# Modulation's last products and the router's set-up moved behind the final norm, its two factors computed in one chain, x parked from ScalarE's queue

## The chip, the core and the metric

The kernel runs on one core of a Trainium2 chip. The metric is the device time of one execution in microseconds (us); a kernel is run several times and the median is given. The core has five engines that run side by side, each with its own instruction stream in a fixed order: TensorE (matrix products, PE, with its weight loads PEld), VectorE (DVE), ScalarE (ACT), GpSimd (POOL) and SyncE (SP). DMA transfers are issued from the queues of SP, ScalarE and GpSimd. [...]

## The reference

All data is float32; 256 tokens of width 1024. A first block has two layers, each with a mixer and a convolutional FFN, and ends with an RMS norm. A second block follows: it is modulated by six vectors from `c`, has a mixer with sparse attention and an RWKV branch, and a mixture of 32 experts. The parts that matter here, shortened:

```
x = x + conv_ffn(rms_norm(x, norm_ffn[1]), ...)        # last FFN of the first block
h = rms_norm(x, norm_final)                             # the final norm
mod = silu(c) @ ada_w + ada_b
sh1, sc1, gt1, sh2, sc2, gt2 = split(mod, 6)
xn = rmsnorm(h, mix_norm_g) * (1 + sc1) + sh1           # the norm that follows at once
proj = xn @ w_in                                        # projections of the second mixer
h = h + gt1 * (merged @ w_out)
xn2 = rmsnorm(h, moe_norm_g) * (1 + sc2) + sh2
h = h + gt2 * hier_moe(xn2, router weights, expert weights)
```

So two norms stand one behind the other: the final norm of the first block, whose result `h` is also the residual of the second block, and the modulated norm before `proj`. `sh2`, `sc2` and `gt2` are needed only behind the second mixer: the first two by the router and the experts, `gt2` when the experts' results are added.

## The kernel before, in words

Tokens lie on the partitions in two tiles of 128 (`x[0]`, `x[1]`), or features lie on the partitions and tokens along the free dimension (`hT`, 8 blocks of 128 features). Large products are made of three fp32r products of a high and a low part each (`mm3`, L272 to L274); the weights are loaded from SP (`load_raw`, L241), and split into the parts by ScalarE and VectorE (`split_act`, L305 and L306).

*The end of the last FFN.* It accumulates in four PSUM banks of the pool `pc`, first the left 512 columns for both token tiles, then the right ones. When a half is complete, `ending` adds it to x (L420), `final_half` multiplies by `norm_final` (L1382) and turns the result into feature blocks on TensorE (L377), and the sums of squares of this product and of x are taken on ScalarE (L334).

*The two norms in one.* `final_norms` makes from the two sums of a token the factor of both norms together: three small instructions (L1396 to L1398) and `newton`, an inverse square root by three Newton steps. It is called for one column at a time, for each of the two token tiles; for one column a step has two instructions (L318, L322), for several columns three (L320, L321, L322). `factor_rows` brings the factors into a row: for each token tile a diagonal (L353, one buffer for both) and a product with ones (L354), then a copy (L355). For each of the 8 feature blocks follow L1407 (VectorE: block by gain by row), L1408 (ScalarE: shift added, rounded to the high part) and L1409 (VectorE: the low part). Last come the two tiles of x itself (L1411), with a factor of their own (`rms`), which the second block needs as its residual.

*Modulation.* The weights of the six vectors are loaded and mostly summed up on VectorE during the first block (`mod_load`). `mod_steps` makes the last products of what is ready: for the shift `sh2` 8 small products for each half (L828) and an addition (L830), for the gate `gt2` one product of one row by 512 columns for each half (L817), an addition of the bias (L818) whose row is loaded from SP into one buffer (L816), and a store of the result (L819). `final_norms` calls it between the Newton steps and `factor_rows`.

*Router's set-up.* `router_setup` loads the router's weights from GpSimd's queue, multiplies them by the shift (8 products, L1523), adds the bias and spreads the row over the partitions (L1524, L1526, L1528), and scales the weights (L1529). It is called between the first block and the second mixer.

*The second mixer.* `second_mixer` closes the PSUM pools and opens others (2, 3 and 3 banks instead of 4 and 4), stores both tiles of x to memory from SP (L1441, the parked x), and starts with the projections: the low-rank inputs of RWKV (`rwkv_low`), the index of the sparse attention, key, receptance and value of RWKV, in between the index mask on VectorE, then `rwkv_prep`.

*What sets the order.* The program above is not the order on the engines. When the kernel is built, a planner orders the instructions of each engine by the time at which it thinks their inputs and places ready, and among ready ones by their position in the program. Instructions stand far from their place in the program: the constant that L1535 makes in `router_setup` is computed at 1.4 us. At run time each engine keeps the planned order and waits where an input is late.

Of the kernel before, what the change touches and what calls it, by code (L numbers as in the profile page):

```python
# [17 lines left out]
NT = 2  # L18
TT = (slice(0, 128), slice(128, 256))
# [71 lines left out]
def view(v, dims, dtype):  # L91
    if dtype not in (F32, F32R):
        v = v.bitcast(dtype)
    names = "abcde"[:len(dims)]
    if len(dims) > 1:
        left = f"({' '.join(names)})"
        v = v.rearrange(f"p {left} -> p {' '.join(names)}", **dict(zip(names, dims)))
    return v


def flat(t):
    n = len(t.shape) - 1
    names = " ".join("abcde"[:n])
    return t.rearrange(f"p {names} -> p ({names})") if n > 1 else t


class Net:
# [1279 lines left out]
    def final_norms(self, p, ss, banks):  # L1387

        nc, x, xg, sg = self.nc, self.x, self.xg, self.sg
        hi, lo = self.hT  # L1390
        stt = nc.vector.scalar_tensor_tensor
        rs = []
        for t in range(NT):

            w, y, u = (self.stile(1, f"rms2_{n}") for n in "wyu")
            nc.vector.tensor_scalar(w, ss[t][0], ss[t][1], 1e-6, op0=ALU.add, op1=ALU.mult)  # L1396
            nc.vector.tensor_scalar(w, w, 1e-12 * D, sg[t][0], op0=ALU.add, op1=ALU.add)
            nc.vector.tensor_scalar(w, w, sg[t][1], 0.5 / D, op0=ALU.add, op1=ALU.mult)  # L1398
            self.newton(y, w, u)
            rs.append(y)  # L1400
        self.mod_steps()
        gcol, shcol = self.mod_cols(0, 1, self.mix_g)
        rows = self.factor_rows(rs, p)
        for k in range(8):
            ps, sh = banks[k // 2][:, k % 2], shcol[:, k:k + 1]
            full = p.tile([128, S], name="full", bufs=2)
            stt(full, ps, gcol[:, k:k + 1], rows, op0=ALU.mult, op1=ALU.mult)  # L1407
            nc.scalar.activation(hi[:, k], full, AF.Identity, bias=sh)  # L1408
            stt(lo[:, k], full, sh, hi[:, k].bitcast(F32), op0=ALU.add, op1=ALU.subtract)  # L1409
        for t in range(NT):  # L1410
            nc.scalar.activation(x[t], xg[t], AF.Copy, scale=self.rms(ss[t]))  # L1411
        p.drop(*list(p.tags))

    def gate(self, gate, i, blocks=range(0, 8, 2)):

        for f in blocks:
            ps = self.psum("pg")
            self.feats([ps], self.w2(2888 + 1024 * i + 128 * f, 256), self.hT)
            self.nc.scalar.activation(flat(gate[:, f:f + 2]), ps, AF.Tanh, scale=0.5)
# [13 lines left out]
    def second_mixer(self):  # L1433
        nc, tc, A, x = self.nc, self.tc, self.A, self.x
        tt, stt = nc.vector.tensor_tensor, nc.vector.scalar_tensor_tensor
        self.open_psum(pg=2, pc=3, ps=3)
        self.ring(0, 4)

        park = self.dram.tile([S, D], F32, name="x_park")
        for t in range(NT):  # L1440
            nc.sync.dma_start(park[TT[t]], x[t])  # L1441
        self.base.drop("x0", "x1")
        self.par1.drop(*list(self.par1.tags))
        with ExitStack() as es:
            E = lambda: es.enter_context(self.scope())
            p, z, pa, pg, pc = E(), E(), E(), E(), E()
            split = lambda n: (lambda y: (y[:, 0], y[:, 1]))(p.tile([128, 2, 4, S], F32R, name=n))
            oa = split("oa")
            room = self.part(p, 10240, "room")
            first, second, third = (Arena(self.af.tiles, room.gaps[0][0] + o, n)  # L1450
                                    for o, n in ((0, 7168), (7168, 3072), (8192, 2048)))
            both = z.tile([128, 4096], name="rw_KRB")
            pb = Scope(self, self.part(pa, 5760, "attention"))
            gates = [pg.tile([128, 8, S], name=f"gate{i}") for i in range(2)]
            qkv, bias = pb.tile([128, 3, 1024], name="qkv"), pb.tile([128, 384], name="bias")
            self.ring(3, 4)
            KR, KB = view(both[:, :2048], (2, 4, S), F32), view(both[:, 2048:], (16, 2, 64), F32)
            v, g, bon = (z.tile([128, 4, S], name=f"rw_{n}") for n in ("v", "g", "bon"))
            with self.scope(first) as zz, self.scope(second) as px:
                sg, k, a = (zz.tile([128, 4, S], name=f"rw_{n}") for n in ("sg", "k", "a"))  # L1460
                self.rwkv_low(sg, a, g, first)
                mask = self.index_mask(px, *self.index_in(px), bias)
                self.rwkv_proj(k, 1, "pg")
                next(mask)
                self.rwkv_proj(KR[:, 1], 0, "pg")
                next(mask)
                self.rwkv_proj(v, 2, "pg")
                fe = self.rwkv_prep(p, zz, KR, KB, bon, k, v, sg, a)
            qT, kT, vn = self.qkv(qkv, third)
            with self.scope(room) as pr:  # L1470
                ops = self.rwkv_pairs(pr, pc, KR, KB)
                z.drop("rw_KRB")
                orw = split("orw")
                self.rwkv_bonus(bon, v)
                self.gate(gates[0], 0, range(0, 8, 2))
                self.rwkv_chain(pc, ops, v, fe, lambda i, Y, junk: self.rwkv_out(i, Y, junk, bon, g, orw))
                self.attention(pb, qT, kT, vn, bias, oa)
                self.gate(gates[1], 1)
                pa.drop(*list(pa.tags))
                for _ in self.branch(A["w_branch_attn_2"][0], oa, gates[0]):  # L1480
                    pass
            pc.drop(*list(pc.tags))
            z.drop("rw_g", "rw_v", "rw_bon")
            p.drop("room", "oa")
            self.par2.drop(*list(self.par2.tags))
            self.ring(8, 4)
            self.x = x = [self.base.tile([128, D], name=f"x{t}") for t in range(NT)]
            for t in range(NT):
                nc.sync.dma_start(x[t], park[TT[t]])
            last = Scope(self, self.part(p, 2 * D, "last"))  # L1490
            gt1 = self.bcast_row(self.mod[0], last.tile([128, D], name="gt1"))
            self.late = [(a, a + n) for a, n in p.tags["last"][1]]
            m = self.hT
            for j in self.branch(A["w_branch_rwkv_2"][0], orw, gates[1]):
                sl = slice(j, j + 2)
                ga, gr = (flat(y[:, sl]) for y in gates)
                tt(ga, ga, gr, ALU.add)
                mh, ml = (flat(y[:, sl]) for y in m)
                nc.scalar.activation(mh, ga, AF.Copy, scale=0.5)
                stt(ml, ga, 0.5, mh.bitcast(F32), op0=ALU.mult, op1=ALU.subtract)  # L1500
            acc = [[self.bank(), self.bank()], [self.bank(), self.psum()]]
            done, ss = self.ending(acc, lambda n: None, gt1, last)
            for i in range(2):
                mi = tuple(y[:, 4 * i:4 * i + 4] for y in m)
                self.out_proj(acc, self.items(mi, A["w_out_2"][0], 4 * i, 4), i == 0, done if i == 1 else None)
            return ss
# [254 lines left out]
def build(nc, tc, A, out):  # L1761
    with ExitStack() as ctx:
        net = Net(nc, tc, ctx, A, out)
        net.first_block()
        net.router_setup()
        ss = net.second_mixer()
        net.finish_blocks()
        net.moe(ss)
# [18 lines left out]
```

## Time and profile before

| | |
|---|---|
| median of 3 runs | 1501.56 us (1499.7 to 1502.51) |
| profiled execution | 1502.12 us, of which the span from the first to the last instruction 1500.4 |
| mean granted clock | 0.950 |
| busy: PE, DVE, ACT, POOL | 1371.2, 852.7, 615.2, 32.2 us |
| end of the last FFN's products | 727.3 us |
| first projection of the second mixer | 740.8 us |
| first expert products | 1047.8 us |

Times in the trace count from the span's start. A row of the timeline gives the start, the duration from the first to the last of merged instructions, the engine, the line of the kernel, the operation, what it writes and reads, shapes, and in brackets how long the engine was idle before it and what ended that. One fp32 product is shown as two records. Tiles are called by their storage: `arena` and `arena_r` hold almost all of them, `pc`, `ps` and `pg` are PSUM.

### The profile page before, as it was taken

The page shows a single profiled execution, that of the slowest core. Times are in us where ns is not written, and L with a number is a line of the kernel's source. Part 1 is how long each engine was busy: PE and PEld are TensorE (multiplying, and loading weights), DVE is VectorE, ACT ScalarE, POOL GpSimd, SP SyncE. Part 2 cuts the span into 40 slices and gives each one's busy share as a digit, 9 for nine tenths or more (in the row PEclk, how much of TensorE's full clock was granted, in tenths as well). Part 3 has the DMA queues.
Part 4 walks back from the last instruction along what each step waited for, and adds up shares of the span by engine and source line. Part 5 has one row for each costly group of instructions (what it writes and reads, how often), then busy time and mean ns, then how long its engine had stood idle before and what let it go on. Part 6 is the DMA issues. An engine that isn't in the chain of part 4 may idle for free.

```text
span 1500.4 us, 22885 instructions
## 1 busy us (share of the span) xinstructions
PE 1371.2 (91%) x9085; PEld 1042.1 (69%) x9085; DVE 852.7 (57%) x1628; ACT 615.2 (41%) x955; POOL 32.2 (2%) x63
## 2 busy tenths in 40 slices
PE   7999999999999899999999899998978878879785
PEld 6778999999998689999798688887413313234131
DVE  5796798778788789878859742775201101101011
ACT  6644555556688555555575544552100000000000
POOL 3000000000001000000000100001000000000000
PEclk9999999999999999999899795999999989999998
DMA  9898586555555578563243352487999999999997
GB/s 318 282 327 277 158 274 215 187 187 160 170 182 184 172 272 275 187 191 109 72 153 113 99 121 86 170 336 308 390 421 420 420 420 421 421 421 419 421 419 253
DMA packets 165573, 391.18 MB, mean 261 GB/s; under 512 B 19440, under 2 KB 101100, under 8 KB 141780
## 3 DMA queue, kind: packets, MB, share of 16 engines
q1 hardware_dynamic: 153124, 383.64, 70.2%
q10 hardware_dynamic: 11136, 4.53, 1.3%
q0 software_dynamic: 1200, 1.49, 0.4%
q8 instruction: 73, 1.20, 0.3%
q14 instruction: 40, 0.33, 0.1%
HBM read 386.19 MB, written 3.43 MB: 260 GB/s over the span
## 4 chain that ended last, share of the span: by engine, by line
PE 58%; DMA 29%; DVE 7%; ACT 4%; issue 2%; SPq 0%; POOL 0%; DVEq 0%; ACTq 0%
DMA arena<-expert_w_gate 12%; PE ps L272 9%; PE ps L273 9%; PE ps L274 9%; DMA arena_w<-expert_w_gate 7%; DMA arena_w<-expert_w_down 6%; PE pc L273 5%; PE pc L272 5%; PE pc L274 5%; DMA arena<-expert_w_down 3%; PE pg L272 2%; PE pg L274 2%; PE pg L273 2%; DVE arena_r L306 2%; ACT arena_r L305 1%
## 5 line engine op out<-in xcount | busy, mean ns | idle before, releaser
L305 ACT ACTIVATE arena_r<-arena 128x1024 fp32r<-128x1024 f32 (+2 forms) x330 | 328.9, 1008 | 287.1 <-PE ps L273 73.1
L306 DVE TENSOR_TENSOR arena_r<-arena,arena_r 128x1024 fp32r<-128x1024 f32 (+2 forms) x330 | 376.9, 1154 | 119.2 <-ACT arena_r L305 115.8
L272 PE MATMUL ps<-arena_r,arena_r 128*128 128x256 f32 (+2 forms) x1192 | 353.7, 297 | 1.0 <-DVE arena L818 1.0
L273 PE MATMUL ps<-arena_r,arena_r 128*128 128x256 f32 (+2 forms) x1192 | 352.9, 296 | 1.1 <-DVE arena_r L306 1.1
L274 PE MATMUL ps<-arena_r,arena_r 128*128 128x256 f32 (+2 forms) x1192 | 352.4, 296 | 0.6 <-DVE arena_r L306 0.6
L272 PEld LDWEIGHTS ps<-arena_r,arena_r 128*128 128x128 f32 (+1 forms) x1192 | 229.3, 192 | 10.4 <-issue 3.5
L273 PEld LDWEIGHTS ps<-arena_r,arena_r 128*128 128x128 f32 (+1 forms) x1192 | 229.2, 192 | 7.2 <-DVE arena_r L306 1.5
L274 PEld LDWEIGHTS ps<-arena_r,arena_r 128*128 128x128 f32 (+1 forms) x1192 | 229.2, 192 | 5.6 <-DVE arena_r L306 0.8
L1709 PE MATMUL pc<-arena 128*32 128x512 f32 x576 | 144.4, 672 | 34.1 <-DMA arena<-expert_w_up 18.9
L272 PE MATMUL pc<-arena_r,arena_r 128*128 128x512 f32 x344 | 136.0, 399 | 5.3 <-ACT arena_r L305 3.4
L273 PE MATMUL pc<-arena_r,arena_r 128*128 128x512 f32 x344 | 135.9, 395 | 0.4 <-DVE arena_r L306 0.4
L274 PE MATMUL pc<-arena_r,arena_r 128*128 128x512 f32 x344 | 134.2, 393 | 0.0
L1709 PE MATMUL pc<-arena_w,arena 128*32 128x512 f32 x448 | 117.4, 663 | 15.8 <-DMA arena_w<-expert_w_gate 9.8
L1716 DVE TENSOR_TENSOR arena<-arena,pc 128x512 f32<-128x512 f32 x8 | 5.5, 688 | 204.6 <-PE pc L1709 204.6
L1692 ACT ACTIVATE arena<-ps,mod_col,moe_g 128x128 f32<-128x128 f32 x32 | 14.7, 458 | 246.1 <-DVE arena L1694 246.1
L1709 PEld LDWEIGHTS pc<-arena 128*32 128x32 f32 x576 | 31.4, 120 | 99.1 <-issue 37.1
L272 PE MATMUL pg<-arena_r,arena_r 128*128 128x256 f32 (+1 forms) x312 | 95.0, 306 | 2.0 <-DVE arena L916 1.8
L273 PE MATMUL pg<-arena_r,arena_r 128*128 128x256 f32 (+1 forms) x312 | 94.7, 305 | 1.1 <-DVE arena_r L306 1.1
L274 PE MATMUL pg<-arena_r,arena_r 128*128 128x256 f32 (+1 forms) x312 | 95.1, 306 | 0.2 <-DVE arena_r L306 0.2
L521 DVE SCALAR_TENSOR_TENSOR arena<-arena 128x255 f32<-128x255 f32 (+2 forms) x228 | 94.4, 477 | 0.2
L1735 PE MATMUL pc<-arena 128*32 128x512 f32 (+2 forms) x320 | 74.7, 584 | 11.5 <-DMA arena<-expert_w_down 7.6
L272 PEld LDWEIGHTS pc<-arena_r,arena_r 128*128 128x128 f32 x344 | 65.2, 190 | 19.8 <-ACT arena_r L305 5.1
(451 smaller groups left out, 1688.2 us busy)
## 6 DMA issues: line engine op xcount, KB each, us to landing
arena<-f_w_up SPq DMA_DIRECT2D x96, 512.0 KB, 3.9
arena<-expert_w_gate SPq DMA_DIRECT2D x41, 1024.0 KB, 19.9
arena<-expert_w_down SPq DMA_DIRECT2D x34, 1024.0 KB, 19.9
arena_w<-expert_w_up SPq DMA_DIRECT2D x33, 1024.0 KB, 19.9
arena<-expert_w_up SPq DMA_DIRECT2D x31, 1024.0 KB, 19.9
arena_w<-expert_w_down SPq DMA_DIRECT2D x26, 1024.0 KB, 19.9
arena<-ada_w SPq DMA_DIRECT2D x48, 512.0 KB, 5.6
arena<-f_w_down SPq DMA_DIRECT2D x48, 512.0 KB, 4.2
```

The lines of the kernel that those rows point to most:

```text
L272: nc.tensor.matmul(acc, ah, bh, start=first, stop=False, **kw)
L273: nc.tensor.matmul(acc, ah, bl, start=False, stop=False, **kw)
L274: nc.tensor.matmul(acc, al, bh, start=False, stop=last, **kw)
L305: self.nc.scalar.activation(hi, src, AF.Copy)
L306: self.nc.vector.tensor_tensor(lo, src, hi.bitcast(F32), ALU.subtract)
L521: nc.vector.scalar_tensor_tensor(o[:, i:], src[:, :S - i], w[k - 1 - i], o[:, i:], op0=ALU.mult, op1=ALU.add)
L1692: nc.scalar.activation(xg[:, k], ps[:, j], AF.Identity, scale=g, bias=sh)
L1709: nc.tensor.matmul(gu[i][es], xg[:, kk, es], ws[e][:, k], start=kk == 0, stop=kk == 7, skip_group_check=True)
L1716: tt(hd, hd, gu[1], ALU.mult)
L1735: nc.tensor.matmul(o[es], hT[:, k0 + k, es], ws[e][:, k, f0 - c0:f0 - c0 + n], start=k0 + k == 0, stop=k0 + k == 3, skip_group_check=True)
```

## The change

Four edits in one. The Newton steps for the two token tiles become one chain over a tile of two columns. `mod_steps` is called at the end of `final_norms`, behind the scaling of x, instead of ahead of `factor_rows`. `router_setup` is called inside `second_mixer`, between the value projection and `rwkv_prep`, instead of ahead of it. The two stores of x are issued from ScalarE instead of SP.

```diff
@@ final_norms
         rs = []
-        for t in range(NT):
-
-            w, y, u = (self.stile(1, f"rms2_{n}") for n in "wyu")
+
+        w2, y2, u2 = (self.stile(NT, f"rms2_{n}") for n in "wyu")
+        for t in range(NT):
+            w = w2[:, t:t + 1]
             nc.vector.tensor_scalar(w, ss[t][0], ss[t][1], 1e-6, op0=ALU.add, op1=ALU.mult)
             nc.vector.tensor_scalar(w, w, 1e-12 * D, sg[t][0], op0=ALU.add, op1=ALU.add)
             nc.vector.tensor_scalar(w, w, sg[t][1], 0.5 / D, op0=ALU.add, op1=ALU.mult)
-            self.newton(y, w, u)
-            rs.append(y)
-        self.mod_steps()
+            rs.append(y2[:, t:t + 1])
+        self.newton(y2, w2, u2)
         gcol, shcol = self.mod_cols(0, 1, self.mix_g)
         rows = self.factor_rows(rs, p)
...
             nc.scalar.activation(x[t], xg[t], AF.Copy, scale=self.rms(ss[t]))
         p.drop(*list(p.tags))
+        self.mod_steps()
@@ second_mixer
         for t in range(NT):
-            nc.sync.dma_start(park[TT[t]], x[t])
+            nc.scalar.dma_start(park[TT[t]], x[t])
...
                 self.rwkv_proj(v, 2, "pg")
+                self.router_setup()
                 fe = self.rwkv_prep(p, zz, KR, KB, bon, k, v, sg, a)
@@ build
         net.first_block()
-        net.router_setup()
         ss = net.second_mixer()
```

## Rows read from the trace of the kernel before

**Rows 1.** The page, chain that ended last: share of the span by engine.
```profile
PE 58%; DMA 29%; DVE 7%; ACT 4%; issue 2%; SPq 0%; POOL 0%; DVEq 0%; ACTq 0%
```
**Rows 2.** Windows: stretch, its us, busy time by engine (records), PEclk, DMA share, GB/s.
```profile
728.90:732.31 3.41, 3.41 (x27) 2.53 (x28) 1.79 (x4) 1.72 (x6) 0.00 (x0) 1.00 0.00 0
732.31:735.72 3.41, 2.52 (x6) 0.41 (x4) 3.38 (x23) 1.10 (x3) 0.00 (x0) 0.50 0.56 150
745.00:780.00 35.00, 35.00 (x269) 33.11 (x267) 19.56 (x36) 25.00 (x44) 0.44 (x2) 0.99 0.44 137
...
1050.00:1055.00 5.00, 5.00 (x52) 1.49 (x48) 0.20 (x2) 0.00 (x0) 0.00 (x0) 1.00 0.50 167
```
**Rows 3.** Timeline from the last FFN's residual to the modulation's second gate product.
```profile
727.33 0.69 DVE L420 TENSOR_TENSOR arena<-arena,pc 128x512 f32<-128x512 f32 x1 [0.74 <-PE pc L274]
...
727.45 1.48 ACT L305 ACTIVATE arena_r<-arena 128x864 fp32r<-128x864 f32 x2
...
727.66 3.55 PE L828 MATMUL pc<-ones,arena 128*64 128x1 f32 x32
729.77 0.15 DVE L830 TENSOR_TENSOR mod_col<-mod_col,pc 64x8 f32<-64x8 f32 x1 [1.76 <-PE pc L828]
729.85 0.68 DVE L1382 TENSOR_TENSOR arena<-arena 128x512 f32<-128x512 f32 x1
...
731.14 1.02 PE L817 MATMUL pc<-arena,ones 128*1 128x512 f32 x2
...
732.53 0.67 DVE L818 TENSOR_TENSOR arena<-arena,pc 1x512 f32<-1x512 f32 x1
...
732.96 1.86 PE L817 MATMUL pc<-arena,ones 128*1 128x512 f32 x2
```
**Rows 4.** Timeline from the Newton steps to the first projection.
```profile
734.41 0.14 DVE L314 TENSOR_SCALAR rms_y<-rms_w 128x1 int32<-128x1 int32 x1
...
736.22 0.28 DVE L353 TENSOR_SCALAR arena<-ident,rms_y 128x128 f32<-128x128 f32 x1
...
736.65 0.77 PE L354 MATMUL pc<-arena,ones 128*128 128x128 f32 x2 [1.82 <-DVE rms_y L322]
...
737.34 1.12 PE L1523 MATMUL pc<-rw,mod_col 128*1 128x36 f32 x16
...
738.39 0.80 PE L354 MATMUL pc<-arena,ones 128*128 128x128 f32 x2
...
739.22 0.61 PE L1526 MATMUL pc<-r_row,ones 1*128 1x36 f32 x2
...
740.03 0.67 DVE L818 TENSOR_TENSOR arena<-arena,pc 1x512 f32<-1x512 f32 x1
...
740.84 0.55 PE L272 MATMUL ps<-arena_r,arena_r 128*128 128x256 f32 x1 [1.01 <-DVE arena L818]
```
**Rows 5.** Timeline of VectorE, the Newton steps over two columns in `qkv`.
```profile
828.58 0.15 DVE L314 TENSOR_SCALAR rs_y<-rs_w 128x2 int32<-128x2 int32 x1
...
829.95 0.16 DVE L322 SCALAR_TENSOR_TENSOR rs_y<-rs_u,rs_y 128x2 f32<-128x2 f32 x1
```
**Rows 6.** Timeline of TensorE, factors and modulation in the first block's second mixer.
```profile
382.94 0.38 PE L354 MATMUL pc<-arena,ones 128*128 128x128 f32 x2
383.15 1.84 PE L822 MATMUL pc<-ones,arena 128*128 128x1 f32 x16
384.93 1.02 PE L817 MATMUL pc<-arena,ones 128*1 128x512 f32 x2
385.88 0.49 PE L354 MATMUL pc<-arena,ones 128*128 128x128 f32 x2
```
**Rows 7.** Windows, the stretch of the index mask.
```profile
780.00:800.00 20.00, 16.81 (x129) 15.48 (x127) 18.10 (x56) 14.04 (x32) 0.00 (x0) 0.93 0.50 158
```
**Rows 8.** Timeline of SP's queue, the second park and the next loads.
```profile
749.41 0.33 SPq L1441 DMA_DIRECT2D x_park<-arena x1
750.80 57.54 SPq L241 DMA_DIRECT2D arena<-w_in  x15
```

## The prediction

> **What bounds the kernel now.** I read the chain that ended last first. TensorE holds 58% of it and DMA 29% [rows 1]: two regimes. The DMA part is the stream of expert weights behind the router. It doesn't start early enough to hide a shift in front of it: at 1050 to 1055 us the DMA engines are half busy, since all places for weights are full until the first expert products free them [rows 2]. So whatever the change gains or loses around 730 to 800 us should reach the end one to one.
>
> Then I read the stretch of the change in the timeline, engine by engine. The last FFN's residual ends at 728.02 (L420, 727.33 + 0.69), and the first projection of the second mixer starts at 740.84 (L272) [rows 3, 4]. In these 12.8 us nothing large is done: sums, a Newton root, the factors turned into a row by two small products (L354), and the first of eight steps L1407 to L1409. The granted clock falls from 1.00 to 0.50 at 732.31, though the engine is shown busy for all of the 3.41 us ahead of it, mostly with the modulation's products L828 [rows 2]. From 745 to 780 us TensorE is shown busy throughout with the projections [rows 2], so there each us of its time is a us of the kernel's.
>
> **The change part by part.**
>
> *Modulation's last products leave their place.* At present L828 fills TensorE's idle time from 727.66 (32 records, 3.55 us). They are free there, but not their ends: VectorE, in order, stands 1.76 us at L830 with L1382 behind it, so L1382 starts at 729.85 instead of 728.02 [rows 3]. With L830 away, the sum over L1382's result can start when ScalarE is through with two splits (727.45 + 1.48 = 728.93), not at 730.53 (L1382's end): 1.6 us gained. L818 (0.67 us) stands directly ahead of L1396 at 732.53; without it the gain is 0 to 0.67, I take 0.6.
>
> Where do they go? The order on each engine isn't the program's: a planner takes what is ready. It doesn't take everything that is ready, though. The router's products L1523 need only what L828 makes, which ends at 731.21 and is added by an instruction of 0.15 us; yet they stand at 737.34, behind the first L354, with TensorE idle for 1.82 us before that [rows 3, 4]. L354 and L1523 draw PSUM banks from one pool, and L354's bank is requested first in the program. I read this as: a bank is not given to a later request before the earlier one has it, and it gets it when its first writer is sent off. Today mod_steps requests its banks ahead of factor_rows; the change turns that round. Then the products can't go ahead of the first L354. What they do behind it is to be seen where the program already has this order: in the second mixer of the first block the first L354 is at 382.94, then 16 records of L822 and a pair L817, and only then, at 385.88, the second L354 [rows 6]. There are two more such places in this trace (at 174.9 and 520.8 us), with the same picture.
>
> So I expect, behind the first L354, the 32 records of L828 and two pairs of L817. Price of the 32: 3.55 us at the full clock. At 0.50 the trace has none of them; the two pairs of L817 lie on both sides of the clock's fall and take 1.02 and 1.86 us, a ratio of 1.82 [rows 2, 3], which would make 6.5 us of the 3.55. I take 5.5, nearer to the upper end, as the clock is at 0.50 there, but below it, as these products load weights more than they stream. A pair of L817 is put at its 1.86 us.
>
> *Factors in one chain.* Two Newton chains of 8 instructions become one of 11, as the product of two columns can't be fused. What counts is the dependent chain: 734.41 to 736.22 is 1.81 us for 8 steps today [rows 4]. A Newton over 2 columns is in the trace: the 1st instruction at 828.58, the 8th at 829.95, 0.196 us a step [rows 5]; 11 steps are 2.16 us. Cost 0.35 us, with bounds of -0.4 (if the neighbours that now interleave were what slowed the 8) and +0.7.
>
> [...]
>
> *Sum up to the first projection.* First L354: 736.65 - 1.6 - 0.6 + 0.35 = 734.8. Then 0.77 for it, 5.5 for L828, 0.8 for the second L354 and 1.86 for one pair of L817, in whatever order: 743.7. From the second L354's start to the first projection it is 2.45 us today (738.39 to 740.84) [rows 4], of which TensorE idles some 1.65; the pair or the rest of L828 fills that and is counted already. So 743.7 against 740.84: +2.9. Bounds: if only 16 records get in and at the full price, 734.8 + 0.77 + 1.8 + 2.45 = 739.8, -1.0; with 6.5 us and both pairs ahead of it, 746.6, +5.7.
>
> *The rest of the modulation.* The second pair of L817 falls among projections that leave no gap: 1.0 us (0 to 1.86).
>
> *Router's set-up.* L1523 (1.12 us) and L1526 (0.61) leave the stretch before the projections [rows 4]; their going is in the sum above, which has no term for them. They come back in the second mixer, near its value projection, where TensorE is mostly full and VectorE has the index mask to do: 0 to 1.7 us, I take 0.4, as TensorE also waits there (it is busy for 16.8 of the 20 us from 780 to 800 [rows 7]). Its loads need nothing of the moved work and stay far ahead.
>
> *x parked from ScalarE.* On SP the second park is issued at 749.41 and the next load only at 750.80 [rows 8]; that load waits for its place, not for the park. Nothing gained. On ScalarE an issue like SP's 0.33 us may stand ahead of the copy of the factor row (L355) or a split: 0 to 0.5, I take 0.2.
>
> Sum: +2.9 + 1.0 + 0.4 + 0.2 = +4.5 us. The profiled execution took 1502.12 us (span 1500.4), 0.56 above the median of the runs; on the median the forecast is 1501.56 + 4.5 = 1506.1, given as 1506.
>
> **The rivals.**
>
> *The order stays (27%).* The planner puts L828 into the idle time at 727.66 again, since nothing else is ready for TensorE. For it: that is where they are now, with a program position already behind the Newton. Against it: L1523. Then the start is as now, the chain costs +0.35, L1523's stretch ahead of the second L354 goes (-0.5), the router comes back with +0.4 and the park with 0.2: about +0.4, 1502 us.
>
> *Faster (15%).* The products are left for later waits of TensorE (3.2 us from 780 to 800 [rows 7] and others) and cost nothing. First L354 at 734.8, the second after 0.77 and the 0.4 that the shared buffer of L353 costs, at 736.0, the projections at 738.4: -2.4; the clock may come back a step sooner, -1; router and park +0.6: -2.8, 1498.8 us. Against it: in none of the three places with this order do they wait.
>
> *A bank held by the gate's row (8%).* The second pair's sum L818 needs a bias row whose one buffer is free only when the first row has been stored: from the first L818 to the second it is 7.5 us today (732.53 to 740.03), and the first projection starts just behind the second, with L818 named as its releaser [rows 3, 4]. If the new pools' banks lie on that one, the projections wait: 743.7 + 0.67 + 7.5 = 751.9, +11: 1512.6 us. It decides when neither of the first two banks of the projections is free of it.
>
> **How the numbers follow.** The forecast has 50%, its own range is +1 to +8 (1502.5 to 1509.5). What a measurement can tell from no change is 0.2%, 3 us: 1498.6 to 1504.6. The forecast lies above in about 39 of its 50 points, within in 11; the order that stays: 3 above, 22 within, 2 below; faster: 4 within, 11 below; the bank: 8 above. Together: slower 0.50, same 0.37, faster 0.13. The range for 8 in 10 leaves out the far ends of the last two rivals: 1499 to 1511.
>
> **What would show it.** Right: behind the first L354 stands L828, the second L354 starts 6 us or more after the first, L1382 directly behind the last L420, the first L272 about 3 us later than now against that L420. Wrong: L828 again directly behind the FFN's last product, or among the projections after 760; L1407 nearer to 737; a wait of the first L272 for L818 over 5 us would be the last rival.

## The result, and the profile after

The changed kernel takes 1511.98 us (median of 4 runs, 1510.99 to 1513.35) against 1501.08 (4 runs): a ratio of 1.0067, 95% interval 1.0054 to 1.008, so 10.9 us slower, where 4.5 was forecast. The direction was right, the size was not. The profiled execution took 1513.35 us with a span of 1511.6, 11.2 more than before's.

The timeline of the changed kernel, from the last residual of the FFN to the first projections (columns as ahead of the prediction):

```profile
729.18 0.69 DVE L420 TENSOR_TENSOR arena<-arena,pc 128x512 f32<-128x512 f32 x1 [0.73 <-PE pc L274]
...
729.90 0.69 DVE L1382 TENSOR_TENSOR arena<-arena 128x512 f32<-128x512 f32 x1
...
733.64 0.16 DVE L314 TENSOR_SCALAR rms_y<-rms_w 128x2 int32<-128x2 int32 x1
...
735.34 1.07 DVE L306 TENSOR_TENSOR arena_r<-arena,arena_r 128x888 fp32r<-128x888 f32 x1
...
736.72 0.28 DVE L353 TENSOR_SCALAR arena<-ident,rms_y 128x128 f32<-128x128 f32 x1
...
737.15 0.77 PE L354 MATMUL pc<-arena,ones 128*128 128x128 f32 x2 [5.84 <-DVE rms_y L322]
...
737.85 3.55 PE L828 MATMUL pc<-ones,arena 128*64 128x1 f32 x32
...
741.32 1.87 PE L817 MATMUL pc<-arena,ones 128*1 128x512 f32 x2
...
743.12 0.80 PE L354 MATMUL pc<-arena,ones 128*128 128x128 f32 x2
743.23 0.68 DVE L818 TENSOR_TENSOR arena<-arena,pc 1x512 f32<-1x512 f32 x1 [1.63 <-PE pc L817]
...
743.85 1.44 PE L817 MATMUL pc<-arena,ones 128*1 128x512 f32 x2
...
743.93 0.25 SPq L819 DMA_DIRECT2D mod<-arena  x1
...
743.95 0.37 ACT L355 COPY arena<-pc 128x256 f32<-128x256 f32 x1 [5.70 <-PE pc L354]
...
744.36 0.88 DVE L1407 SCALAR_TENSOR_TENSOR arena<-ps,arena 128x256 f32<-128x256 f32 x2 [0.46 <-ACT arena L355]
...
745.08 0.24 SPq L816 DMA_DIRECT2D arena<-ada_b  x1
...
748.86 0.67 DVE L818 TENSOR_TENSOR arena<-arena,pc 1x512 f32<-1x512 f32 x1
...
749.67 0.55 PE L272 MATMUL ps<-arena_r,arena_r 128*128 128x256 f32 x1 [4.39 <-DVE arena L818]
```

Read it from below. TensorE has stood idle for 4.39 us before the first projection (L272), released by the second L818: that addition reads the PSUM bank which the second pair of L817 filled, and the new pools give the same bank to the first projection. L818 is late because of its bias row, but not in the way that the rows suggest. The row's one buffer is free only when the first row is stored: L818 at 743.23, its store (L819) at 743.93, the load of the next row (L816) at 745.08. By the record of the load's semaphore in the trace that row has landed at 746.38, though, and the queue of VectorE passes the wait for it at 748.2 within 21 ns. From 746.38 on L818 waits for its turn: the planner has put six L1407 and four L1409, work of the feature blocks, ahead of it, and e3 below shows that it does so because of the one buffer. The chain that ended last, in order of time, runs over this work and not over the load (start, us):

```profile
747.27 0.88 DVE arena_r L1409 x2
...
748.47 0.47 DVE arena L1407
748.94 0.59 DVE arena L818
...
749.67 0.55 PE ps L272
```

Above that stand the moved products, all between and behind the two L354. Counted from the last L420 the first projection comes 20.49 us later (749.67 - 729.18); before, it was 13.51 (740.84 - 727.33) [rows 3, 4]. That is +6.98.

Where the rest of the 11.2 us lies: I subtracted the start of each TensorE product in the trace of before from that of the same product here. 1.9 us are there ahead of any edited instruction: 1.0 by 25 us, where the profile's first record of the clock, at 1.00, is at 17.7 us instead of 15.5 (products of 512 columns follow each other in 0.43 us ahead of it and in 0.23 behind it), and 0.9 at 490 us, where the granted clock is 0.50 from 488.7 to 492.1 and 1.00 before the change. Then +6.95 at the norm. In the mask's stretch it rises by another 1.7 and falls back, +0.6 left at 860 us. From there to the last expert product little changes (+9.4 at 860 us, +9.3 at 1490), so this part of the stream hides nothing. The last 1.8 us are behind the last addition. Views: before, then after; the last addition and the span.

```profile
1491.55 0.51 DVE L1744 TENSOR_TENSOR arena<-arena,ps 128x128 f32<-128x128 f32 x2 [0.58 <-PE ps L1743]
```
```profile
core 0 of [0], span 1511.6 us
...
1500.89 0.51 DVE L1746 TENSOR_TENSOR arena<-arena,ps 128x128 f32<-128x128 f32 x2 [0.58 <-PE ps L1745]
```

From there to the end it is 8.3 us before (1500.4 - 1492.06) and 10.2 after. Without the 1.9 us in which the two executions differ before the change begins, 9.3 us are placed, of the 10.9 of the medians.

### The profile page after: what moved, and what is told of

Same layout as the page of the kernel before. It is cut to its first block, busy times and chain, and to the rows that moved or that the text cites. A ratio compares the mean times of both kernels' runs of the same rounds, so it can differ in the third digit from the quotient of the medians.

```text
span 1511.6 us, 22875 instructions
## 1 busy us (share of the span) xinstructions
PE 1368.6 (91%) x9085; PEld 1041.8 (69%) x9085; DVE 852.3 (56%) x1623; ACT 615.5 (41%) x955; POOL 32.2 (2%) x63
## 4 chain that ended last, share of the span: by engine, by line
PE 57%; DMA 28%; DVE 8%; ACT 4%; issue 2%; SPq 0%; POOL 0%; DVEq 0%; ACTq 0%
DMA arena<-expert_w_gate 12%; PE ps L272 9%; PE ps L273 8%; PE ps L274 8%; DMA arena_w<-expert_w_gate 7%; DMA arena_w<-expert_w_down 6%; PE pc L272 5%; PE pc L273 5%; PE pc L274 5%; DMA arena<-expert_w_down 3%; DVE arena_r L306 2%; PE pg L272 2%; PE pg L274 2%; PE pg L273 2%; ACT arena_r L305 1%
## 5 line engine op out<-in xcount | busy, mean ns | idle before, releaser
L306 DVE TENSOR_TENSOR arena_r<-arena,arena_r 128x1024 fp32r<-128x1024 f32 (+2 forms) x330 | 376.7, 1154 | 123.7 <-ACT arena_r L305 118.8
L272 PE MATMUL ps<-arena_r,arena_r 128*128 128x256 f32 (+2 forms) x1192 | 354.1, 297 | 4.4 <-DVE arena L818 4.4
L273 PE MATMUL ps<-arena_r,arena_r 128*128 128x256 f32 (+2 forms) x1192 | 353.2, 296 | 1.0 <-DVE arena_r L306 1.0
L274 PE MATMUL ps<-arena_r,arena_r 128*128 128x256 f32 (+2 forms) x1192 | 352.8, 296 | 0.6 <-DVE arena_r L306 0.6
L272 PEld LDWEIGHTS ps<-arena_r,arena_r 128*128 128x128 f32 (+1 forms) x1192 | 229.5, 193 | 15.0 <-ACT arena_r L1408 5.7
L273 PEld LDWEIGHTS ps<-arena_r,arena_r 128*128 128x128 f32 (+1 forms) x1192 | 229.6, 193 | 7.0 <-DVE arena_r L306 1.4
L274 PEld LDWEIGHTS ps<-arena_r,arena_r 128*128 128x128 f32 (+1 forms) x1192 | 229.6, 193 | 5.6 <-DVE arena_r L306 0.8
L1711 PE MATMUL pc<-arena 128*32 128x512 f32 x576 | 140.1, 647 | 36.3 <-DMA arena<-expert_w_up 21.1
L272 PE MATMUL pc<-arena_r,arena_r 128*128 128x512 f32 x344 | 137.0, 402 | 5.3 <-ACT arena_r L305 3.3
L273 PE MATMUL pc<-arena_r,arena_r 128*128 128x512 f32 x344 | 136.7, 397 | 0.0
L274 PE MATMUL pc<-arena_r,arena_r 128*128 128x512 f32 x344 | 135.4, 397 | 0.0
L272 PE MATMUL pg<-arena_r,arena_r 128*128 128x256 f32 (+1 forms) x312 | 94.8, 306 | 2.0 <-DVE arena L916 1.8
L274 PE MATMUL pg<-arena_r,arena_r 128*128 128x256 f32 (+1 forms) x312 | 95.1, 306 | 0.2 <-DVE arena_r L306 0.2
L273 PE MATMUL pg<-arena_r,arena_r 128*128 128x256 f32 (+1 forms) x312 | 94.4, 304 | 0.4 <-DVE arena_r L306 0.4
L272 PEld LDWEIGHTS pc<-arena_r,arena_r 128*128 128x128 f32 x344 | 65.8, 191 | 19.9 <-ACT arena_r L305 5.0
## 6 DMA issues: line engine op xcount, KB each, us to landing
arena_w<-expert_w_down SPq DMA_DIRECT2D x26, 1024.0 KB, 19.7
```

The lines of the kernel that those rows point to most:

```text
L272: nc.tensor.matmul(acc, ah, bh, start=first, stop=False, **kw)
L273: nc.tensor.matmul(acc, ah, bl, start=False, stop=False, **kw)
L274: nc.tensor.matmul(acc, al, bh, start=False, stop=last, **kw)
L306: self.nc.vector.tensor_tensor(lo, src, hi.bitcast(F32), ALU.subtract)
L1711: nc.tensor.matmul(gu[i][es], xg[:, kk, es], ws[e][:, k], start=kk == 0, stop=kk == 7, skip_group_check=True)
```

## Experiments

Five executions of each kernel or more, in turns with the kernel before; the interval is that of the ratio. Distances are from the last L420 to the first projection: 13.5 us in the kernel before, 20.5 in the changed one. Line numbers shift by a few where a diff adds lines.

**e1: the moved products alone.** The kernel before with:

```diff
-        self.mod_steps()          # ahead of factor_rows
...
+        self.mod_steps()          # end of final_norms
```

> The kernel before with one edit of the four: mod_steps moved behind the final norm. Theory (a bank held): the products stand behind the first L354, the second L354 stands 6 us behind the first, the first projection waits for the second L818, whose bias row can be loaded only when the first has been stored; the router's products L1523 and L1526 fit into that wait. So nearly the whole loss: 8 to 10 us over before, 1509 to 1511 us, the first projection 20 to 21 us behind the last L420 (13.5 before). Rival (the four edits share the loss): under +5 us, 1506 or less.

1514.47 against 1501.96: 1.0082 (1.0068 to 1.0096), +12.5, more than expected. The order is as in the theory, with the first L272 at 21.4 us:

```profile
731.68 0.77 PE L354 MATMUL pc<-arena,ones 128*128 128x128 f32 x2 [3.88 <-DVE rms_y L322]
...
747.11 0.55 PE L272 MATMUL ps<-arena_r,arena_r 128*128 128x256 f32 x1 [5.29 <-DVE arena L818]
```

This edit alone makes the loss at the norm.

**e2: the products back, the other three edits kept** (the changed kernel with the diff of e1 turned round).

> The changed kernel with mod_steps put back ahead of the factor rows, the other three edits kept. Theory: the loss goes; the router's products have left the stretch ahead of the projections (0.5 to 1 us gained) and come back around 800 us (up to 1.7 us lost): 1500 to 1503 us, first projection 12 to 13.5 us behind the last L420. Rival (the other edits carry a part of the loss): 1505 or more.

1507.41 against 1501.96: 1.0037 (1.0025 to 1.005). The distance is 13.7, as the theory has it, but the time is 5.4 us above before, as the rival has it. In the profiled execution 0.4 us of that are at the norm, 2.6 arise where the clock is still at 0.50 and that of the kernel before is back at 1.00, and 1.7 behind the last addition (10.0 us to the end instead of 8.3). Windows, before and e2 (columns as in [rows 2]):

```profile
933.70:940.50 6.80, 6.80 (x94) 5.92 (x93) 1.39 (x2) 4.07 (x10) 0.00 (x0) 1.00 0.01 2
```
```profile
933.70:940.50 6.80, 6.80 (x71) 6.00 (x69) 0.69 (x1) 1.96 (x5) 0.00 (x0) 0.50 0.01 2
```

So the parts don't add up (12.5 and 5.4 against 10.9), and the next runs look for what the three other edits do.

**e5, e6, e11: each of the three alone** (router_setup in second_mixer; one chain; x parked from ScalarE).

> The kernel before with the router's set-up moved into the second mixer, nothing else. The changed kernel with mod_steps put back was still 5.4 us slower than before, where I had expected nothing; its profile is level with before to 725 us, +0.3 behind the norm, +1.8 at 780 to 825, +0.8 at 880 us, +3.5 from 930 us. Theory (what is left of the loss comes from the router's place and from the clock's fall at 900 to 940 us): 1504 to 1507. Rival (the chain or the park carry it): the move is worth what I had put it at, 0.4 us, or gains the 0.5 us of the stretch it leaves: 1501 to 1503.

> The kernel before with the factors in one chain, nothing else. Theory: one chain of 11 with another norm's root and a weight split in between is 0.5 to 1.3 us longer up to the first L354, and the second L354 keeps its distance: 1502 to 1503.5. Rival (it carries what was left of the loss with mod_steps put back): 1505 or more.

> The kernel before with x parked from ScalarE's queue, nothing else. Theory: hidden, as the two issues (0.4 and 0.33 us in the changed kernel) stand where ScalarE waits: 1501 to 1503. Rival (ScalarE's queue holds up splits or the copy of the factors): 1504 or more.

Router 1505.72 against 1502.40, 1.0019 (1.0011 to 1.0028); chain 1505.50, 1.0017 (1.0007 to 1.0026); park 1504.69 against 1501.02, 1.0024 (1.0015 to 1.0033). Each some 3 us, none where I looked for it. At the norm the router's move gains 0.3 (13.2) and the park nothing (13.5); the chain costs 1.0 (14.5). In the profiled executions of the first two most of the rest is in the clock. Windows of the index mask's stretch, in before, with the router moved, with one chain, with the park (us, busy by engine, granted clock, DMA):

```profile
775.00:830.00 55.00, 50.71 (x371) 46.22 (x370) 47.85 (x133) 32.36 (x60) 0.00 (x0) 0.97 0.42 131
```
```profile
775.00:830.00 55.00, 51.67 (x373) 47.73 (x373) 46.69 (x127) 31.92 (x59) 0.00 (x0) 0.91 0.40 121
```
```profile
775.00:830.00 55.00, 51.81 (x371) 48.02 (x369) 44.17 (x120) 33.01 (x60) 0.00 (x0) 0.91 0.42 125
```
```profile
775.00:830.00 55.00, 50.70 (x364) 45.66 (x363) 48.52 (x135) 32.64 (x60) 0.00 (x0) 0.97 0.46 132
```

The records of the clock in the traces of before and of the changed kernel have two values alone, 0.50 and 1.00; if the same holds here, 0.91 instead of 0.97 is 6.6 us more at 0.50 (0.06 x 55 x 2), by my estimate 3.3 us of full clock; by 860 us the products of the router's kernel start 3.1 us later than before's, and at 775 they were level within 0.3. TensorE waits for the mask's work there (L1258, 1.4 us in before); why the clock is lower, no run shows. In the changed kernel it is 0.97, as before. The chain's profiled execution (1510.90) is the slowest of its 11, 5.4 us above their median, so its shares say little of the median. With the park alone the first projection keeps its distance, but the planner has another order behind it: three L272 stand first, where L272, L273 and L274 stood, and VectorE and ScalarE have work moved beside them. Its profiled execution, the fastest of its 12, shows no loss by that, only the longer end, 10.5 us instead of 8.3. For the 3.7 us of its median I have no more than that.

**e3: a second buffer for the bias row.**

```diff
-                row = self.mod_scope.tile([1, 512], name="mrow")
+                row = self.mod_scope.tile([1, 512], name="mrow", bufs=2)
```

> The changed kernel with two buffers for the gate's bias row, so that the second row needn't wait until the first is stored. Theory: the second L818 follows its products at once, the 4.4 us wait of the first L272 for it goes, first projection about 16 us behind the last L420 instead of 20.5: 1507 to 1509 us. Rival (the feature blocks of L1407 to L1409, or the products themselves, set the start anyway): the wait moves to L1408 or L1409 and at most 1 us comes back, 1511 to 1513.

1509.37 against 1501.96: 1.0047 (1.0034 to 1.0061), 2.6 us under the changed kernel (3 by the ratios), distance 19.5. The wait of TensorE for L818 is gone, but it comes back in another place:

```profile
742.78 1.86 PE L817 MATMUL pc<-arena,ones 128*1 128x512 f32 x2
...
742.89 0.37 ACT L355 COPY arena<-pc 128x256 f32<-128x256 f32 x1 [5.70 <-PE pc L354]
...
744.68 0.67 DVE L818 TENSOR_TENSOR arena<-arena,pc 1x512 f32<-1x512 f32 x1 [1.85 <-PE pc L817]
...
745.28 0.86 DVE L1407 SCALAR_TENSOR_TENSOR arena<-ps,arena 128x256 f32<-128x256 f32 x2
...
746.35 1.01 PE L272 MATMUL ps<-arena_r,arena_r 128*128 128x256 f32 x3 [1.70 <-ACT arena_r L1408]
```

With the row there in time, the second L818 is ordered ahead of the first L1407 and VectorE stands 1.85 us at it; the factor row (L355) was ready at 743.26. The rival was right on this point: the products themselves also hold up the start.

Only 1.0 us of the gain is at the norm. More arises where nothing was meant to change: against the kernel before, the products stand 9.1 us late at 920 us and 5.4 at 1000; in the changed kernel it is 9.4 and 9.2. The second row moves other tiles within `arena`, the engines run another order from 895 to 990 us, and the clock is back at 1.00 earlier (granted 1.00 instead of 0.50 from 936.4 to 942.5). Every kernel below that is cut in two has this second row as well.

**e9, e10: half of the products back.** `mod_steps` gets an argument for which vectors it takes; e9 leaves the shift (L828) behind the norm, e10 the gate (L817, L818):

```diff
+        self.mod_steps(only=(5,))     # e10: (3,)
         gcol, shcol = self.mod_cols(0, 1, self.mix_g)
...
-        self.mod_steps()
+        self.mod_steps(only=(3,))     # e10: (5,)
```

> The changed kernel with the gate's products (L817, L818 and the bias rows) put back ahead of the factor rows and only the shift's 32 records (L828) left behind the norm. Theory (the wait for the second gate row is the large term, the shift's products the small one): only L828's 3.55 us stands between the two L354, nothing waits for L818; first projection 14.5 to 16 us behind the last L420 (20.5 in the changed kernel, 13.7 with both put back): 1506 to 1509. Rival (the shift's products are the large term): first projection at 18 or later, 1510 or more.

> The changed kernel with the shift's products put back ahead of the factor rows and only the gate's two pairs (L817, L818) left behind the norm. Theory: the chain first L818, store, load of the second bias row, second L818 still takes 5.6 us and the first projection waits for it; first projection 18.5 to 20 us behind the last L420: 1509 to 1512. Rival (without the shift's products the gate's rows are done in time): 17 or less, 1506 or less.

e9: 1509.15 against 1501.02, 1.0053 (1.0039 to 1.0066). e10: 1512.71, 1.0067 (1.0053 to 1.008). With the shift late the distance is 14.0: the 3.55 us of L828 stand between the two L354 and almost nothing is lost by it. With the gate late the first projection starts at 15.7, into one bank, and the next, into another, waits (L820 is L818 there):

```profile
744.37 0.38 PE L272 MATMUL ps<-arena_r,arena_r 128*128 128x256 f32 x1
...
747.69 0.67 DVE L820 TENSOR_TENSOR arena<-arena,pc 1x512 f32<-1x512 f32 x1
...
748.41 0.42 PE L272 MATMUL ps<-arena_r,arena_r 128*32 128x256 f32 x1 [2.77 <-DVE arena L820]
```

It goes on 19.7 us behind the last L420, nearly where the changed kernel does. So at the norm the gate's row is nearly the whole loss. In the medians it is less clear: e9 is 8.1 us above before, e2, with nothing left behind the norm, 5.4. In e9's profiled execution 3.2 us arise in the mask's stretch, at a granted clock of 0.91, and 1.8 behind the last addition.

**e4, e7: cut in two.** `mod_steps` makes only the products ahead of the factor rows (both halves of the shift in one bank, two bias rows) and hands its additions and stores to the end of `final_norms`. e4 is the changed kernel with this. e7 is the kernel before with it, and there the additions also multiply by a one that is made from the Newton result, so that they can't be ordered ahead of it:

```diff
+        one = self.stile(1, "one")
+        nc.vector.tensor_scalar(one, rs[1], 0.0, 1.0, op0=ALU.mult, op1=ALU.add)
         rows = self.factor_rows(rs, p)
...
+        for end in later:
+            end(one=one)
```

> The changed kernel with mod_steps cut in two: its products ahead of the factor rows (the halves of the shift in one bank, two bias rows), its additions and stores at the end of final_norms. Theory: the products stand in TensorE's idle time behind the FFN again, no L354 and no projection waits for them or for the bias row: 1498 to 1501 us, first projection 11 to 13 us behind the last L420. Rival (VectorE still stands at the shift's addition ahead of the last L1382, so nothing is gained over the order of before): 1501 to 1503.

> The kernel before, with mod_steps cut in two: the products stay ahead of the factor rows (the halves of the shift in one bank, two bias rows), the additions are made to depend on the Newton result by a factor of one taken from it, so that VectorE can't stand at them ahead of the last L1382 and the sums. Theory: L1382 directly behind the last L420, first L354 7 to 8 us behind that L420 (9.3 before), first projection 11 to 12 (13.5): 1498.5 to 1500.5. Rival (the feature blocks or the additions in front of them set the start as before): within 1 us of before.

e4: 1504.33 against 1501.96, 1.0015 (1.0006 to 1.0024): as its rival had it, and 1 us more: VectorE still stood at the shift's addition ahead of the last L1382, and the first projection is 15.3 us behind the last L420, where 11 to 13 were expected. e7: 1494.33 against 1502.40, 0.994 (0.9928 to 0.9952), 8.1 us faster than before, four more than I had worked out. In its trace the first L354 is 7.1 us behind the last L420 (9.3 before) and the distance 12.6. But little of its gain is at the norm: against before its products stand 2.1 us late ahead of the norm and 1.7 behind it, 2.8 late at 920 us, 1.6 early at 1000 and 7.8 early at 1480. The step from 920 to 1000 us is as in e3, which has the second bias row too; the other lies in the stream of expert weights, which no edit touches.

**e8, e12: the same cut with the router moved, and in the changed kernel.**

> As the gated kernel, with the router's set-up moved into the second mixer as well. Theory that the router's place costs: 2 to 5 us slower than the gated kernel. Rival (the router's place costs nothing, its going frees the stretch ahead of the projections): level with it or up to 1 us faster.

> The changed kernel (one chain, router and park as changed) with the gated cut of mod_steps: products ahead of the factor rows, additions behind the Newton steps. Theory (the place of the products is what costs; router and chain cost little once it is free): 1493 to 1497, near the two gated kernels. Rival (chain and router cost 3 us each as they did alone): 1498 to 1502.

1494.58 against 1502.40, 0.9948 (0.9935 to 0.9961); 1494.90 against 1501.02, 0.995 (0.9936 to 0.9964). Both are within 1.5 us of e7 by the ratios: here router, chain and park cost nothing that shows.

**e13, e14, e15, e17: order or address.** The new tile `one` moves the large tile `arena`, which holds most weights, by 64 bytes in each partition, from byte 25536 to 25600. e13 is the kernel before with an unused tile of that size, every engine's order unchanged; e14 is e7 without a new tile (the one is written into a scratch tile); e15 is the changed kernel with the unused tile; e17 is e13 with `arena` 68 words smaller, so that the eight weight places behind it begin on a multiple of 512 bytes too.

```diff
+        self.small.tile([128, 1], F32, tag="pad", name="pad", bufs=2)    # e13, e15, e17
...
-    F_WORDS, R_TILES = 34500, 8
+    F_WORDS, R_TILES = 34432, 8                                          # e17
```

> The kernel before with one unused small tile, which moves arena by 64 bytes in SBUF (from byte 25536 of a partition to 25600); the order of every engine is the same. Theory (the address makes the weight stream faster): the stretch from 1100 to 1400 us moves 426 GB/s instead of 420, 1494 to 1497 us. Rival (the gated order did it): 1501 to 1503, 420 GB/s.

> The gated kernel (e7) with its factor of one written into a scratch tile that is there already, so that arena lies where it does in the kernel before. Theory (the address gave most of the 8 us): 420 GB/s from 1100 to 1400 us, what stays is the earlier first projection, 1 to 2.5 us: 1499 to 1501. Rival (the order of the work gave it): 1494 to 1496.

> The changed kernel with the same unused small tile, arena moved by 64 bytes. Theory (address and order add up): 5 to 7 us faster than the changed kernel, 1505 to 1507; first projection still 20 us behind the last L420. Rival: 1511 to 1513.

> The kernel before, the same order on every engine, with arena at byte 25600 and 68 words smaller, so that all weight places behind it begin on a multiple of 512 bytes too. Theory (the address alone, from e13's 5.5 us and e16's 4 us over e7): 8 to 10 us faster than before, 1492 to 1495; the gated order (e16, 1490.2) keeps 2 to 4 us over it. Rival (the gain of e16 over e7 was the order or the clock): level with e13, 1496 to 1498.

e13: 1497.21 against 1502.76, 0.9966 (0.9952 to 0.9979). e14: 1499.06, 0.9975 (0.9964 to 0.9986). e15: 1506.67, 1.0026 (1.0016 to 1.0036). e17: 1496.07 against 1503.13, 0.9956 (0.9942 to 0.997). Windows of the weight stream, in before, e13 and e17 (last column: GB/s):

```profile
1100.00:1400.00 300.00, 243.74 (x1194) 92.74 (x1190) 39.34 (x76) 13.60 (x30) 0.00 (x0) 0.94 1.01 420
```
```profile
1100.00:1400.00 300.00, 240.86 (x1195) 91.56 (x1192) 39.35 (x76) 14.19 (x31) 0.00 (x0) 0.96 1.01 425
```
```profile
1100.00:1400.00 300.00, 242.18 (x1194) 92.48 (x1192) 39.38 (x76) 14.12 (x31) 0.00 (x0) 0.95 1.01 427
```

The address alone is worth 5.5 us, in e17 7.1 (the theory had hoped for 8 to 10). The cut with its second bias row, and `arena` in its place, is worth 3.7 (e14, at 421 GB/s). Its order at the norm (L838, L844 and L827 are L828, L830 and L818 there, L1396 is L1382):

```profile
728.60 3.55 PE L838 MATMUL pc<-ones,arena 128*64 128x1 f32 x32
...
728.82 0.68 DVE L420 TENSOR_TENSOR arena<-arena,pc 128x512 f32<-128x512 f32 x1
...
730.39 0.69 DVE L1396 TENSOR_TENSOR arena<-arena 128x512 f32<-128x512 f32 x1
...
735.59 0.46 PE L354 MATMUL pc<-arena,ones 128*128 128x128 f32 x2 [0.52 <-DVE rms_y L322]
...
736.48 0.22 DVE L844 SCALAR_TENSOR_TENSOR mod_col<-pc,rms_u,mod_col 128x8 f32<-128x8 f32 x1
...
736.68 0.73 DVE L827 SCALAR_TENSOR_TENSOR arena<-pc,rms_u,arena 1x512 f32<-1x512 f32 x1
...
741.08 0.55 PE L272 MATMUL ps<-arena_r,arena_r 128*128 128x256 f32 x1 [1.42 <-DVE r_add L1547]
```

The products run beside the last L420 again, and no addition stands ahead of L1382 or the factors: the first L354 is 6.8 us behind L420 (9.3 before), the first projection 12.3 (13.5). This profiled execution is the slowest of e14's seven (1502.26); its products gain 2.1 us at the norm and 1.6 from 920 to 1000 us, the second row's stretch, and lose 2.8 in the mask's, at a granted clock of 0.91. So how much of the 3.7 us is the cut's and how much the second row's is not shown. With the same new address the changed kernel is 9.5 us behind (e15 less e13), with the distance at 20.5 as ever: the loss at the norm is the same at both addresses.

**e16, e18: what the runs point to.** e7 and e12 with the smaller `arena`.

> The gated kernel (e7) with arena 68 words smaller, so that the eight tiles behind it (arena_w, the other weight places) begin on a multiple of 512 bytes as arena does there. Theory (the begin of a place within 512 bytes sets what a transfer costs): the weight stream gets faster again, 1486 to 1492. Rival (only arena's begin counts, or something else that moved with it): level with e7, 1493 to 1496.

> The changed kernel (one chain, router and park as changed) with the gated cut of mod_steps and all places aligned. Theory (with the products back in TensorE's idle time the other three edits cost nothing that can be measured): level with e16, 1489 to 1492. Rival (they cost 3 us as each did alone): 1492.5 to 1496.

e16: 1490.17 against 1502.76, 0.9921 (0.9907 to 0.9934), 12.6 us faster than before and the fastest of all. e18: 1493.97 against 1503.13, 0.994 (0.9927 to 0.9954), some 3 us short of it by the ratios, as its rival had it. In e16's trace only 0.2 us are gained at the norm (distance 13.3), 4.3 from 920 to 1000 us and 7.7 in the weight stream; in that of e17, with the order of before, 7.0 in the stream alone. So what e16 has over e17 in these traces is mostly the second row's stretch, not the cut at the norm.

## Why the prediction was wrong

By its own steps:

- *The change lies on the path to the end, one to one.* Right: the products stand 9.4 us later at 860 us and 9.3 at the last of them.
- *A bank is not given to a later request before the earlier one has it*, so the products can't go ahead of the first L354. Right: L828 and both pairs stand behind it, and the second L354 starts 5.97 us after the first (6 or more forecast).
- *L1382 directly behind the last L420.* Right: 0.72 us behind it, 2.52 before. The first L354 gained 1.35 us by that (7.97 behind L420, 9.32 before) of the 1.85 forecast.
- *Factors in one chain, +0.35.* Too small, though not for the chain's own length. Alone (e6) it puts the first L354 0.8 us later: the 11 steps take 2.23 us (736.25 to 738.48), 0.42 more than the 8 before, and they start 0.37 later behind the last L420, as the one chain needs the sums of both token tiles. In the changed kernel a split of 1.07 us (L306) stands inside the chain. That 16 instructions became 11 shows no gain in e6; what counted there is the longer dependent chain and its later start.
- *L828 at 5.5 us.* Wrong: 3.55 us, at a granted clock of 0.50, the same as before at 1.00 [rows 2, 3]:

```profile
737.92:741.30 3.38, 3.38 (x32) 3.38 (x32) 0.44 (x2) 0.33 (x1) 0.00 (x0) 0.50 1.01 401
```

The ratio of 1.82 was taken from L817, which streams 512 columns and keeps to it (1.87 us a pair here, 1.02 at the full clock); L828 streams one column for each load of weights, and the weight loads are busy all the time (3.38 of 3.38 us).

- *"The second pair of L817 falls among projections that leave no gap: 1.0 us."* This step failed. The pair stands ahead of the first projection, 1.44 us, and its bank isn't free until L818 has read it, which stands behind six L1407 and four L1409 in VectorE's order: another 4.39 us. From the second L354 to the first projection it is 6.55 us instead of the 2.66 of the sum (0.8 + 1.86). With L828 2 us cheaper and the chain 0.5 dearer, 16.4 us became 20.5.
- *The rival "a bank held by the gate's row", 8%, +11.* It came about. I named its place and the chain, and a reading that spoke for it: the first projection was released by L818 in the kernel before too [rows 4]. What I lacked was a reason for its low chance: only one place in the pools had to lie on that bank. e10 shows how near it was: there the first projection's bank is free, the second's isn't, and the wait comes 4 us later all the same. Its price was right in sum only. From L818 to L818 it is 5.6 us and not 7.5, and neither is the row's way alone: the row landed 3.15 us behind the first L818 (746.38), the other 2.5 us are the second L818's place on VectorE. In the kernel before the row landed at 737.75, 5.2 us behind the first L818, and the addition came 2.3 us later. The total came to 11 with 1.9 us of clock ahead of the change and 1.8 at the end. The mark that I set, a wait of over 5 us, was met in e1 (5.29) and missed here by 0.6.
- *Router, +0.4.* 0.6 in the profiled execution; *park, +0.2*: its two issues stand where ScalarE waits anyway, for 0.72 and for 5.70 us. In other executions and kernels the stretch behind costs up to 3.3 us, by my estimate from the clock (e5, 0.91 instead of 0.97 from 775 to 830 us).

What stays open: why three edits that move the start of the projections by 1 us or less each cost some 3 us alone and 5.4 together, 3 in e18, and nothing that shows in e8 and e12. The profiled executions show places, not causes. One is the mask's stretch, by the clock (3 us with the router moved and with one chain, granted 0.91 there instead of 0.97). The second begins at 896 us before, where the clock is at 0.50 for 37.5 us; it stays there for 44.4 us in e2, e6, e10 and e15, which costs 2.6 to 2.7 us each, and for 30.7 in e3, e7, e8 and e16. The third lies behind the last addition (2 us of the park's). With one profiled execution for each kernel I can't say how steady any of them is.

## What to carry to other kernels

Before small work is moved behind a critical step, list what it holds until it is done, PSUM banks and single buffers, who takes those places next, and where their last reader stands in its engine's order: the work itself was cheap, but the last reader of its bank, put late on VectorE for the sake of one buffer, set the start of the next stage. If work lies in idle time of one engine but its follow-up blocks another, leave it there and make only the follow-up depend on something later; in e14 the first projection came 1.2 us sooner by that. And a kernel compared at a few parts in a thousand should keep its large tiles where they were, or be compared with a copy in which nothing but the address moved (5.5 us in e13). One more buffer moves them, too (e3).

## What the runs showed of the hardware

- With the same order on every engine, the weight stream from 1100 to 1400 us ran at 420 GB/s with `arena` at byte 25536 of a partition (before), at 425 with it at 25600 (e13) and at 427 with it at 25600 and 68 words smaller (e17). The places behind `arena` begin at 163552 before, 163616 in e13 and 163328 in e17. Why is not shown: 25600 and 163328 are multiples of 512, as was supposed for e16 and e17, and the others aren't even of 128, so smaller multiples fit these runs as well; no run tells them apart.
- From the last addition to the program's end it is 9.8 to 10.5 us in seven of the kernels and 7.8 to 9.3 in the others, without an instruction of the kernel in it that differs. The seven (the changed kernel, e1, e2, e9, e10, e11 and e15) have one bias row and, with it, the late products or the park on ScalarE's queue; none of the others has both. No run here tells why.
- Single executions differ by some microseconds: 23 runs of the kernel before beside e5 to e8 spread from 1500.22 to 1507.13. In the profiles the stretch from 775 to 830 us had a granted clock of 0.91 to 0.97.
